# Attention of an encoder block with the keys instead of the queries on the partitions

## The chip, the cores and the metric

The kernel runs on one NeuronCore of a Trainium2 chip. Five engines work side by side and meet through semaphores: TensorE (PE in the rows; its weight loads are PEld), VectorE (DVE), ScalarE (ACT), GpSimd (POOL) and SyncE (SP), which only issues DMAs. The metric is the device time of one execution in microseconds, the median of several.

## What is computed

One layer over two independent sequences, a sample of 2048 tokens and a prompt of 256, all in float32, with 1024 columns. Cut to what matters:

```python
hdn = rmsnorm(x, norm_pre)
u, b_gate, c_gate, z_conv, q_lat, kv_lat, k_pe, z_attn = split(hdn @ w_in)
conv_out = b_gate * short_conv(c_gate * u) * silu(z_conv)            # 512 columns
q = rmsnorm(q_lat) @ w_uq        # 8 heads of 64 + 32 columns, the 32 rotated
k, v = rmsnorm(kv_lat) @ w_ukv   # 8 heads of 64 + 64; the 32 rotated key columns are shared
sc = q @ k.T / sqrt(96)          # per head and sequence
o = softmax(sc) @ v * silu(z_attn)
y = x + rmsnorm(concat(conv_out, o) @ w_out, norm_post)
```

## The kernel before

It works in four parts.

**Phase 1** (`phase1`) makes the latents, the convolution branch and the attention's gate. Its products are float32r, in three passes: each operand is cut into a rounded part and a rest, and `mm3` (L87 to 93) adds hi*hi, lo*hi and hi*lo.

**Phase 2** (`Phase2.run`, L531) goes through nine chunks of 256 tokens, the prompt first. Each chunk makes keys, values and queries from the latents with float16 parts, in PSUM groups of 256 columns (keys 4, queries 6) or 512 (values 2), cuts each result into two float16 parts (`split`: ScalarE L71, then VectorE L72) and stores both to DRAM scratch with DMAs on SP: keys (L567, and L594 for the rotated rows, copied to all heads), values (L597), queries (L567). `Heads.load` (L634 on) reads a head's operands back.

**Attention** (`attention`, L655 on) takes 130 units one after the other: two for the prompt, then, head by head, 128 queries of the sample against all 2048 keys. `step(n)` (L847 on) writes the order out by hand (`manual_schedule`): scores of unit n, parts of units n-1 and n-2, value products of the pair of units six steps back (`LAG`). In a unit:

- `scores`: 12 float16 products of 512 columns with the queries on the partitions, into one PSUM tile of 1024 columns and two of 512; VectorE takes the maxima (L695) and forms their negative in one column (L700, L701);
- `exponents`: ScalarE's exponentials with that column as bias, and the row sums (L717), into float32 tiles `p`;
- `upper`, `lower`: `p` is cut into two float16 parts `fp`, by POOL (L756, L759), ScalarE (L758) and VectorE (L765);
- L771: a DMA turns both parts round, into `tt` with the keys on the partitions;
- `values`: 2 float16 products (L775, L776) of 256 columns for each 128 keys and pair of units. The weights are the value's two parts side by side, 128 columns; the stream is the exponentials' first, then second part. `finish` adds the two halves (L833, L839) and stores.

One over the sums goes to DRAM as rows (`spread`, L742 to 747).

**Phase 4** (`Phase4`) is the output projection, for 18 tiles of 128 tokens in two halves of 512 columns, 24 float32r products each (L955, L957). Before that the attention's rows are scaled with the gate and the sums (L935, L937) and cut (L939, L941). Its first halves run between the last steps of the attention.

The exponentials come out with the queries on the partitions, and everything from `upper` to L771 is there to turn them for the value products:

```python
nc.scalar.activation(p, s, AF.Exp, bias=sm[:, 0:1], scale=g.exps[:, 0:1], accum_out=sums[h][:, i, u : u + 1])
```

Of the kernel before, what the change touches and what calls it, by code (L numbers as in the profile page):

```python
# [10 lines left out]
F32 = mybir.dt.float32  # L11
# [28 lines left out]
BIG = 2.0**15  # L40
# [3 lines left out]
LN_BIG = float(np.log(BIG))  # L44
# [3 lines left out]
GROUP, LAST = 4, 2  # L48
LAG = 6
CUT = 384  # L50
# at which step of a head what of the next one is loaded
LOADS = {3: ("k", 0, 1024), 5: ("k", 1024, TS), 7: ("q", 0, 1024), 9: ("q", 1024, TS), 11: ("v", 0, 1024), 13: ("v", 1024, TS)}
# [11 lines left out]
def split(nc, hi, lo, src, scale=None):  # L64
    """hi is src rounded to the products' type, lo what is left; scale goes on both."""
# [21 lines left out]
def mm3(nc, out, terms, first=True, last=True):  # L87
    """float32 products from parts: hi*hi + hi*lo + lo*hi."""
# [7 lines left out]
def rstd(g, r, ssq, n):  # L96
    """r = (ssq / n + eps) ** -0.5 on a column."""
# [5 lines left out]
def phase1(g, x, x_t, w_e, w_lat, npre, convw, open_phase2):  # L103
    """Norm, latents, the conv branch and the attention's gate."""
    nc, tc = g.nc, g.tc
    with ExitStack() as ctx:
# [15 lines left out]
        # The products take x times the norm's weights; a token's scale goes on what comes out of them.  # L122
# [43 lines left out]
        def spread(hf):  # L166
            """The scales of a half's tokens along the free axis, on every partition."""
# [8 lines left out]
        def latents(tiles, between=lambda k: None):  # L176
            """Products of some tokens' tiles, normalised."""
# [64 lines left out]
        def etile(n):  # L242
# [3 lines left out]
            for ci in range(3):  # L246
# [13 lines left out]
                # columns of cu: the sample's end and the prompt's start lie a zero apart  # L260
# [34 lines left out]
        def conv(hf, j, ci):  # L295
            # output tokens of this step: those whose right neighbour is there
# [7 lines left out]
            for a, b in spans:  # L304
                # column of token a in cu
# [79 lines left out]
class Phase2:  # L385
    """Queries, keys and values from the latents, 256 tokens at a time, the prompt first.

    They are stored as two float16 parts each, after powers of two that bring them within the type's range:
    one over what goes on a query's row goes on the key's, but for a factor that is the same for all rows.
    """  # L390

    N = 256

    def __init__(self, g, table):
# [3 lines left out]
        self.turn = 3  # L398
# [255 lines left out]
def attention(g, hd, ps1):  # L654
# [106 lines left out]
    def lower(n, b):  # L761
# [4 lines left out]
        if b == 0:  # L766
            return
# [385 lines left out]
```

## Time and profile before

| | us |
|---|---|
| median of 3 runs | 1746.72 (1746.57 to 1747.05) |
| the profiled execution, its span | 1753.0 |
| PE busy, weight loads busy | 1577.4, 1254.1 |
| DVE, ACT, POOL busy | 1085.1, 821.2, 787.3 |
| phase 1 | 0 to 644.4 |
| phase 2, until its last product | 644.4 to 761.5 |
| attention, until its last scores | 761.5 to 1523.0 |
| overlap of its end with phase 4 | 1523.0 to 1559.3 |
| phase 4 alone | 1559.3 to 1753.0 |

The profile holds one execution. Its only time of its own is the span from the first to the last instruction, 6.3 us above the median of the timed runs. Busy shares of the whole span mix stages with different limits, so they are read stage by stage. A matmul's busy time is longer than the distance to the next one, since matmuls are pipelined: what a product costs in a row of products is the distance between two starts.

### The profile page before, as it was taken

The numbers are of one execution on the slowest core, as the hardware profiler recorded it, in microseconds if no ns is written. First come the engines' busy times: TensorE is split into PE (matmuls) and PEld (weight loads), VectorE is DVE, ScalarE is ACT, GpSimd is POOL, SyncE is SP. The second block draws the span as 40 slices with busy tenths as digits, with TensorE's granted clock in tenths as the row PEclk, the third lists the DMA queues.
The fourth block names the chain that finished last, engine by engine and source line by source line (L and its number), as shares of the span: only waits on it lengthen the run. The fifth ranks groups of instructions, "written<-read, shape, count | busy, mean of one in ns | idle before, by whom it ended". The sixth has DMA issues, their size and how long they took to land.

```text
span 1753.0 us, 24925 instructions
## 1 busy us (share of the span) xinstructions
PE 1577.4 (90%) x9168; PEld 1254.1 (72%) x9168; DVE 1085.1 (62%) x1679; ACT 821.2 (47%) x1596; POOL 787.3 (45%) x785
## 2 busy tenths in 40 slices
PE   8999999999999999978788788888887887889998
PEld 8999999999999997644444444445454444567886
DVE  4333332322444435588799999899999999823333
ACT  7521112452112223367676777677766767612221
POOL 3221121131322113346667676677767677722232
PEclk9999999999999999999899999999999999989999
DMA  9921112543212239999999999999999999994663
GB/s 285 287 78 42 58 50 89 159 108 125 82 60 86 83 114 243 268 197 215 200 209 218 212 221 196 224 205 229 206 224 190 222 206 214 203 226 154 191 192 109
DMA packets 695503, 301.45 MB, mean 172 GB/s; under 512 B 570322, under 2 KB 665428, under 8 KB 695380
## 3 DMA queue, kind: packets, MB, share of 16 engines
q1 hardware_dynamic: 676164, 271.53, 69.4%
q10 hardware_dynamic: 19216, 28.32, 6.4%
q8 instruction: 72, 1.18, 0.3%
q14 instruction: 51, 0.42, 0.1%
HBM read 108.84 MB, written 48.74 MB: 90 GB/s over the span
## 4 chain that ended last, share of the span: by engine, by line
PE 55%; DVE 30%; DMA 7%; ACT 3%; POOL 2%; issue 2%; ACTq 0%; SPq 0%; DVEq 0%; POOLq 0%
DVE mx L695 12%; PE o L91 10%; PE o L93 9%; PE o L92 9%; DVE fp L765 9%; PE out L955 7%; DVE sm L700 7%; DMA tt<-fp 5%; PE out L957 3%; PE pq L91 1%; PE pq L92 1%; PE pq L93 1%; ACT p L717 1%; PE o L775 1%; DMA k_s<-krp 1%
## 5 line engine op out<-in xcount | busy, mean ns | idle before, releaser
L717 ACT ACTIVATE p<-s,sm,exps 128x512 f32<-128x512 f32 (+1 forms) x384 | 348.6, 914 | 184.6 <-DVE sm L701 167.9
L759 POOL TENSOR_TENSOR fp<-p,fp 128x640 f16<-128x640 f32 x260 | 377.4, 1471 | 11.9 <-ACT fp L758 1.1
L775 PE MATMUL o<-tt,v 128*128 128x256 f16 x1024 | 253.8, 285 | 115.5 <-DVE res L839 113.1
L695 DVE TENSOR_REDUCE mx<-s 128x1 f32<-128x512 f32 (+1 forms) x384 | 320.4, 856 | 17.3 <-PE s L93 16.4
L91 PE MATMUL o<-hdn_hi,whi 128*128 128x384 f32 x960 | 323.7, 337 | 0.0
L92 PE MATMUL o<-hdn_lo,whi 128*128 128x384 f32 x960 | 322.7, 336 | 0.0
L93 PE MATMUL o<-hdn_hi,wlo 128*128 128x384 f32 x960 | 322.6, 336 | 0.0
L776 PE MATMUL o<-tt,v 128*128 128x256 f16 x1024 | 252.6, 284 | 0.0
L765 DVE TENSOR_TENSOR fp<-p,fp 128x384 f16<-128x384 f32 x260 | 236.3, 909 | 12.8 <-POOL fp L756 12.6
L756 POOL TENSOR_SCALAR fp<-p 128x1024 f16<-128x1024 f32 x130 | 143.6, 1105 | 219.5 <-ACT p L717 143.1
L91 PE MATMUL s<-k,q 96*128 96x512 f16 (+1 forms) x528 | 210.9, 399 | 28.2 <-ACT p L717 25.1
L776 PEld LDWEIGHTS <-v 128*128 128x128 f16 x1024 | 104.5, 102 | 168.5 <-issue 136.9
L93 PE MATMUL s<-k,q 96*128 96x512 f16 (+1 forms) x528 | 211.0, 400 | 0.0
L92 PE MATMUL s<-k,q 96*128 96x512 f16 (+1 forms) x528 | 209.9, 398 | 0.0
L91 PEld LDWEIGHTS o<-hdn_hi,whi 128*128 128x128 f32 x960 | 180.5, 188 | 0.5
L92 PEld LDWEIGHTS o<-hdn_lo,whi 128*128 128x128 f32 x960 | 180.5, 188 | 0.0
L93 PEld LDWEIGHTS o<-hdn_hi,wlo 128*128 128x128 f32 x960 | 180.5, 188 | 0.0
L758 ACT ACTIVATE fp<-p 128x1024 f16<-128x1024 f32 x130 | 137.4, 1057 | 29.7 <-DMA tt<-fp 26.2
L955 PE MATMUL out<-wo,o_cut 128*128 128x512 f32 x576 | 144.0, 403 | 7.9 <-ACT o_cut L939 7.5
L775 PEld LDWEIGHTS <-v 128*128 128x128 f16 x1024 | 104.0, 102 | 49.4 <-issue 10.7
L700 DVE SCALAR_TENSOR_TENSOR sm<-mx 128x1 f32<-128x1 f32 x128 | 132.4, 1034 | 4.5
L955 PEld LDWEIGHTS out<-wo,o_cut 128*128 128x128 f32 x576 | 109.2, 191 | 34.5 <-ACT o_cut L939 8.2
(222 smaller groups left out, 2227.9 us busy)
## 6 DMA issues: line engine op xcount, KB each, us to landing
w<-in_w_e_dram SPq DMA_DIRECT2D x40, 512.0 KB
x<-in_x_dram SPq DMA_DIRECT2D x18, 512.0 KB
out_dram<-yt SPq DMA_DIRECT2D x36, 256.0 KB
xt<-in_x_t_dram SPq DMA_DIRECT2D x5, 1536.0 KB
o_raw<-mix_s SPq DMA_DIRECT2D x15, 512.0 KB
o_raw<-in_x_dram SPq DMA_DIRECT2D x15, 512.0 KB
lat_s<-lt SPq DMA_DIRECT2D x6, 960.0 KB
lt<-lat_s SPq DMA_DIRECT2D x9, 640.0 KB
```

Source lines behind the costliest of these rows:

```text
L91: nc.tensor.matmul(out, sh, mh, start=first and i == 0, stop=False)
L92: nc.tensor.matmul(out, sh, ml, start=False, stop=False)
L93: nc.tensor.matmul(out, sl, mh, start=False, stop=last and i == n - 1)
L695: nc.vector.reduce_max(mx[:, at : at + 1], s, axis=AX.X)
L700: nc.vector.scalar_tensor_tensor(sm[:, 8:9], mx[:, 0:1], mx[:, 2:3], mx[:, 3:4], op0=ALU.max, op1=ALU.max)
L717: nc.scalar.activation(p, s, AF.Exp, bias=sm[:, 0:1], scale=g.exps[:, 0:1], accum_out=sums[h][:, i, u : u + 1])
L756: nc.gpsimd.tensor_scalar(hi, p, 1.0, 1.0, op0=ALU.mult, op1=ALU.mult)
L759: nc.gpsimd.tensor_tensor(lo[:, CUT:], p[:, CUT:], hi[:, CUT:], op=ALU.subtract)
L765: nc.vector.tensor_tensor(lo[:, :CUT], p[:, :CUT], hi[:, :CUT], op=ALU.subtract)
L775: nc.tensor.matmul(o, v, moving[0], start=first, stop=False)
L776: nc.tensor.matmul(o, v, moving[1], start=False, stop=last)
L955: nc.tensor.matmul(o, mh[:, k, :], wk[k // 2][:, k % 2, w], start=k == 0 and wk is hi, stop=False)
```

## The change

The attention is written anew, and the stages around it follow.

- **Phase 2** makes the keys of all chunks first (after the prompt's keys and queries), then two chunks of queries, then all values, then the other queries. Values stay in SBUF as float32 (`g.v`), with no parts and no way through DRAM. The prompt's attention, and the maxima of the first group, run between the groups of the values and the later queries.
- **Attention**: a group is 512 queries of two heads (16 groups), a step is 128 keys of them (256 steps). `scores` forms the products with the keys on the partitions: 6 float16 products of 512 columns, 3 for each head, into a 1024-column tile. The softmax's maximum is a 97th row of the queries (its partner in the keys is a row of 2^14), so the exponential needs no bias and comes out ready for the value products.
- **Maxima** of group n+1 are taken during group n, from the products of the operands' first parts alone: 32 more products of 512 columns for a group, 2 or 3 in a step, each into one of two PSUM banks (`m`) and reduced by VectorE. `max_rows` turns them into rows with 8 products of 128 columns, which ScalarE copies into the queries.
- **Value products** are float32, one for each head and 128 keys, 64 weight columns and 512 columns of stream, one head's result on partitions 0 to 63, the other's on 64 to 127. They are issued for four steps together.
- **Sums**: POOL adds up the exponentials over the steps (`total`); two float32 products with ones bring the sums onto the partitions of the result, VectorE inverts them, and gate and sums are applied in the attention (`finish`), not in phase 4.
- **Phase 4** starts when the attention ends, takes whole tiles of 1024 columns, and loads and cuts only.

```diff
 class Attention:
+    def max_chunks(self, n):
...
+        for u in range(8):
+            i, b = divmod(u, 4)
+            for c in range(4):
+                m = g.narrow(f"m{n}_{u}_{c}", "m")
+                nc.tensor.matmul(m, q[:DQK, i, 0, b * P : (b + 1) * P], k[:DQK, i, 0, c * 512 : (c + 1) * 512], start=True, stop=True)
+                nc.vector.reduce_max(mx[:, u, c : c + 1], m, axis=AX.X)
+                yield
+    def max_rows(self, n):
...
+            for b in range(4):
+                nc.tensor.matmul(m[:KR, b * P : (b + 1) * P], mst[:, (4 * i + b) % 8, :KR], self.ident, start=True, stop=True)
...
+            nc.scalar.activation(dst, src.rearrange("p (h t) -> p h t", t=TP) if n == "p" else src, AF.Copy)
+    def scores(self, s, k, q, pieces):
+        o = g.wide(f"s{s}")
+        for cols, ki, qi, ks in pieces:
+            nc.tensor.matmul(o[:, cols], k[:KR, ki, 0, ks], q[:KR, qi, 0, :], start=True, stop=False)
+            nc.tensor.matmul(o[:, cols], k[:DQK, ki, 0, ks], q[:DQK, qi, 1, :], start=False, stop=False)
+            nc.tensor.matmul(o[:, cols], k[:DQK, ki, 1, ks], q[:DQK, qi, 0, :], start=False, stop=True)
+    def exponents(self, s, o):
+        p = self.p[s] = self.ps.tile([P, 1024], F32, tag="p", bufs=6, name=f"p{s}")
+        nc.scalar.activation(p, o, AF.Exp, scale=g.exps[:, 0:1])
+    def total(self, key, first, second=None):
...
+            nc.gpsimd.tensor_tensor(self.acc[key], self.acc[key], first, op=ALU.add)
+    def finish(self, key, j, cols):
...
+            nc.tensor.matmul(r[i * DV : (i + 1) * DV, :w], self.ones, acc[:, i * w : (i + 1) * w], start=True, stop=True)
+        nc.scalar.activation(rs, r[:, :w], AF.Copy)
+        yield
+        for i in range(0, w, P):
+            nc.vector.reciprocal(rs[:, i : i + P], rs[:, i : i + P])
...
+        nc.vector.tensor_tensor(res, o[:, :w], gate, op=ALU.mult)
+        nc.sync.dma_start(g.mix[CW + j * P : CW + (j + 1) * P, cols], res)
+    def step(self, s):
...
+        o = self.scores(s, self.k[j], self.q[n], pieces)
+        for _ in range(3 if kt % 4 == 0 else 2):
+            next(self.ahead, None)
+        if n < last:
+            if kt == KT - 3:
+                next(self.ahead, None)
+                self.max_columns(n + 1)
+            if kt == KT - 2:
+                self.max_rows(n + 1)
+        if s % BATCH == 1:
+            self.values(range(max(s - BATCH, 0), s))
...
+        self.exponents(s, o)
+        if kt == 1:
+            self.total(n, self.p[s - 1], self.p[s])
+        elif kt:
+            self.total(n, self.p[s])
+        self.settle()
+    def values(self, steps):
...
+                nc.tensor.matmul(self.o[n][i * DV : (i + 1) * DV], g.v[:, kt, h * DV : (h + 1) * DV], p[:, i * 512 : (i + 1) * 512], start=kt == 0, stop=kt == KT - 1)
...
-            nc.gpsimd.tensor_tensor(lo[:, CUT:], p[:, CUT:], hi[:, CUT:], op=ALU.subtract)
-        nc.vector.tensor_tensor(lo[:, :CUT], p[:, :CUT], hi[:, :CUT], op=ALU.subtract)
-        nc.sync.dma_start_transpose(dst, parts.pop(n).rearrange("p w k -> p (w k)"))
-        nc.tensor.matmul(o, v, moving[0], start=first, stop=False)
-        nc.tensor.matmul(o, v, moving[1], start=False, stop=last)
```

In the middle of the attention, PE's row before (`s65` are scores of unit 65, `o58` the outputs of the pair 58 and 59):

```order
L93 MATMUL s65_0_10739<-k_3_9094,q_3_9093 128x512
L775 LDWEIGHTS v_3_9095
L775 MATMUL o58_10702<-tt58_10476,v_3_9095 128x256
L776 LDWEIGHTS v_3_9095
L776 MATMUL o58_10702<-tt58_10476,v_3_9095 128x256
L775 LDWEIGHTS v_3_9095
L775 MATMUL o58_10702<-tt58_10476,v_3_9095 128x256
L776 LDWEIGHTS v_3_9095
L776 MATMUL o58_10702<-tt58_10476,v_3_9095 128x256
```

and PE's row after, at step 5 (`s5`, `s6` are scores of steps, `m1` products for the next group's maxima, `p1` to `p4` exponentials of steps 1 to 4):

```order
L778 LDWEIGHTS k_0_6296
L778 MATMUL s5_7596<-q_0_6482,k_0_6296 128x512
L741 LDWEIGHTS q_1_7485
L741 MATMUL m1_3_0_7603<-k_0_6296,q_1_7485 128x512
L741 LDWEIGHTS q_1_7485
L741 MATMUL m1_3_1_7606<-k_0_6296,q_1_7485 128x512
L885 MATMUL o0_7538<-p1_7541,v_5674 64x512 x2
L885 MATMUL o0_7538<-p2_7558,v_5674 64x512 x2
L885 MATMUL o0_7538<-p3_7574,v_5674 64x512 x2
L885 MATMUL o0_7538<-p4_7593,v_5674 64x512 x2
L776 LDWEIGHTS k_0_6296
L776 MATMUL s6_7620<-q_0_6482,k_0_6296 128x512
```

Value products no longer stand in eights between a unit's scores: eight float32 ones follow every fourth step's scores and maxima, and carry their weight loads in themselves.

VectorE's row before, one unit (`mx` maxima, `sm` their column, `fp` the float16 parts):

```order
L765 TENSOR_TENSOR fp53_10144<-p53_0_10129,fp53_10144 128x384
L695 TENSOR_REDUCE mx55_10187<-s55_0_10189 128x1
L765 TENSOR_TENSOR fp53_10144<-p53_1_10130,fp53_10144 128x384
L695 TENSOR_REDUCE mx55_10187<-s55_1_10213 128x1
L695 TENSOR_REDUCE mx55_10187<-s55_2_10214 128x1
L700 SCALAR_TENSOR_TENSOR sm55_10188<-mx55_10187 128x1
L701 TENSOR_SCALAR sm55_10188<-sm55_10188,exps_75 128x1
L839 TENSOR_TENSOR res46_2_10096<-o48_10152,top48_3_10233 64x256
```

and after, in the second group's steps 7 to 10 (`m2` products for the third group's maxima, `rsum0` the first group's sums):

```order
L742 TENSOR_REDUCE mx2_7826<-m2_3_3_7956 128x1
L808 RECIPROCAL rsum0_7944<-rsum0_7944 128x128
L742 TENSOR_REDUCE mx2_7826<-m2_4_0_7970 128x1
L742 TENSOR_REDUCE mx2_7826<-m2_4_1_7973 128x1
L808 RECIPROCAL rsum0_7944<-rsum0_7944 128x128
L742 TENSOR_REDUCE mx2_7826<-m2_4_2_7987 128x1
L742 TENSOR_REDUCE mx2_7826<-m2_4_3_7990 128x1
L742 TENSOR_REDUCE mx2_7826<-m2_5_0_7993 128x1
```

The parts, the columns for the bias and the sum of halves have left VectorE; reductions and inversions stay.

SP's row before, one chunk of phase 2 (`sk`, `krp`, `sv`, `sqp`, `sq` are its keys, rotated keys, values, rotated queries, queries):

```order
L567 DMA k_s_67<-sk4_6366 64x8x256 x2
L594 DMA k_s_67<-krp4_6417 32x8x256 x2
L597 DMA v_s_68<-sv4_6407 128x8x256
L567 DMA q_s_66<-sqp4_6368 32x4x256 x4
L567 DMA q_s_66<-sq4_6432 64x8x256 x2
```

and after, in the stretch of the keys (chunks 3 to 5; the rows have no queries between them):

```order
L568 DMA tb5_32_6085<-in_table_dram 32x2x256
L586 DMA kp5_6087<-kpe_s_61 32x256
L601 DMA k_s_66<-krp3_6008 32x8x256 x2
L576 DMA k_s_66<-sk3_5990 64x8x256 x2
L601 DMA k_s_66<-krp4_6061 32x8x256 x2
L576 DMA k_s_66<-sk4_6043 64x8x256 x2
L601 DMA k_s_66<-krp5_6114 32x8x256 x2
L576 DMA k_s_66<-sk5_6095 64x8x256 x2
```

The stores of all keys now follow one another, the stores of the values are gone.

## Rows read from the trace of the kernel before

**Rows 1.** Busy us by engine, granted clock and DMA share, in five stretches.
```profile
core 0: us, PE busy (x) PEld busy (x) DVE busy (x) ACT busy (x) POOL busy (x), PEclk, DMA share, GB/s
0.00:644.40 644.40, 638.18 (x3804) 635.96 (x3804) 228.42 (x379) 188.52 (x371) 140.73 (x251) 1.00 0.35 111
644.40:761.50 117.10, 105.93 (x836) 82.41 (x835) 69.08 (x193) 48.91 (x123) 37.73 (x51) 0.99 0.96 253
761.50:1523.00 761.50, 617.27 (x3572) 363.86 (x3570) 705.38 (x986) 534.62 (x1002) 542.40 (x406) 0.93 1.12 211
1523.00:1559.30 36.30, 28.76 (x129) 22.31 (x129) 15.01 (x22) 9.23 (x18) 12.64 (x11) 0.86 1.22 215
1559.30:1753.00 193.70, 187.26 (x832) 149.57 (x832) 67.18 (x100) 39.93 (x86) 53.75 (x67) 0.99 0.53 167
```
**Rows 2.** Groups by line and shape, VectorE, 800 to 1500: busy us, mean ns.
```profile
L765 DVE TENSOR_TENSOR fp<-p,fp 128x384 f16<-128x384 f32 x236 | 212.8, 902 | 5.9 <-POOL fp L756 5.9
L695 DVE TENSOR_REDUCE mx<-s 128x1 f32<-128x512 f32 x236 | 152.5, 679 | 15.2 <-PE s L93 14.6
L695 DVE TENSOR_REDUCE mx<-s 128x1 f32<-128x1024 f32 x118 | 142.9, 1211 | 0.9 <-PE s L93 0.7
L700 DVE SCALAR_TENSOR_TENSOR sm<-mx 128x1 f32<-128x1 f32 x118 | 124.7, 1057 | 4.2
```
**Rows 3.** Waits, 800 to 1500: us in total, times, longest.
```profile
ACT p L717 <- DVE sm L701: 161.8, 97, 3.0
PE o L775 <- DVE res L839: 113.1, 58, 5.4
```
**Rows 4.** Chain that ended last, phase 4: start, us, sixteen products of one half.
```profile
1735.38 3.74 PE out L955 x16
```
**Rows 5.** Timeline of PE in a unit's scores: start, us, instruction.
```profile
1100.37 0.38 PE L91 MATMUL s<-k,q 96*128 96x512 f16 x1
1100.59 0.38 PE L92 MATMUL s<-k,q 96*128 96x512 f16 x1
```
**Rows 6.** Timeline of PE around the prompt's value products, 64 weight columns.
```profile
779.17 0.38 PE L93 MATMUL s<-k,q 96*128 96x512 f16 x1
779.48 0.30 PE L91 MATMUL o<-tt,v 128*64 128x256 f16 x1
...
780.70 0.27 PE L93 MATMUL o<-tt,v 128*64 128x256 f16 x1
780.90 0.39 PE L91 MATMUL s<-k,q 96*128 96x512 f16 x1
```
**Rows 7.** Groups by shape, ScalarE's exponentials of 1024 columns, 800 to 1500.
```profile
L717 ACT ACTIVATE p<-s,sm,exps 128x1024 f32<-128x1024 f32 x119 | 142.1, 1194 | 0.0
```
**Rows 8.** Groups by shape, VectorE's inversions, 800 to 1753.
```profile
L731 DVE RECIPROCAL rs<-rs 128x16 f32<-128x16 f32 x7 | 1.8, 253 | 0.2
L731 DVE RECIPROCAL rs<-rs 128x4 f32<-128x4 f32 x1 | 0.2, 178 | 0.0
```
**Rows 9.** Groups by shape, POOL's two-operand passes over float32, whole span.
```profile
L941 POOL TENSOR_TENSOR o_cut<-o_raw,o_cut 128x1024 fp32r<-128x1024 f32 x18 | 43.5, 2416 | 140.7 <-ACT o_cut L939 140.7
L1053 POOL TENSOR_TENSOR wo<-stw,wo 128x512 fp32r<-128x512 f32 x16 | 22.4, 1400 | 0.0
```
**Rows 10.** Groups by shape, PE in phase 2: a third of the queries', of the keys'.
```profile
L91 PE MATMUL q<-lt,uq_hi 128*128 128x256 f16 x162 | 44.9, 277 | 7.9 <-DVE sv L72 5.8 <-DVE sqr L543 1.9
L91 PE MATMUL k<-lt,uk_hi 128*128 128x256 f16 x72 | 19.6, 273 | 3.3 <-DVE sq L72 3.3
```
**Rows 11.** Timeline of SP in phase 2: start, us to issue, which DMA.
```profile
706.25 0.59 SPq L529 DMA_DIRECT2D kp<-kpe_s  x1
706.93 1.25 SPq L567 DMA_DIRECT2D k_s<-sk  x2
708.28 2.06 SPq L594 DMA_DIRECT2D k_s<-krp  x2
```
**Rows 12.** Chain that ended last: a load of phase 4, until its data are there.
```profile
1550.10 5.36 DMA o_raw<-mix_s
```

More of the change, by code (lines that the diff above doesn't have):

```diff
@@ new lines, in queries @@
+                    yield "q", ci, m
+            last = len(self.chunks)
+            self.load(1, pb, "q")
+            yield from keys(0)
+            yield from queries(0)
+            self.load(2, pb, "q")
+            for ci in range(1, last):
+                yield from keys(ci)
+            for ci in (1, 2):
+                yield from queries(ci)
+                self.load(ci + 2, pb, "q")
+            for ci in range(last):
+                yield from values(ci)
+            for ci in range(3, last):
+                yield from queries(ci)
+                if ci + 2 < last:
+                    self.load(ci + 2, pb, "q")
@@ L905, in __init__, with load @@
         self.ready = {}
[L906 to L911 removed]
+    def load(self, i):
+        nc = self.g.nc
         sl = slice(i * P, (i + 1) * P)
[L913 to L926 removed]
@@ L1032, in tile_encoder, with beside @@
-    hd.load(0, "v", 1536, TS)
-    hd.load(0, "q", 1536, TS)
-    g.pb = pool("p3b", bufs=2)
+    side = []
+    def beside():
+        yield from at.max_chunks("p")
+        at.max_columns("p")
+        yield
+        at.max_rows("p")
+        yield
+        first = at.max_chunks(0)
+        rest = [at.prompt(j) for j in range(H // 2)]
+        live = [rest.pop(0)]
+        for i, _ in enumerate(first):
+            yield
+            if i % 2 == 0 and live:
+                if next(live[0], at) is at:
+                    live.pop(0)
+                    live += rest[:1]
+                    del rest[:1]
+        at.max_columns(0)
+        yield
+        at.max_rows(0)
+        yield
+        for w in live + rest:
+            for _ in w:
+                yield
@@ L1035, in tile_encoder @@
+    for _ in between:
+        pass
     pwo = pool("p4w", bufs=1, side="right")
@@ L1101, in tile_encoder @@
-    for n in range(NU, NU + LAG + 1):
-        step(n, more=more)
-    while halves:
-        more()
+    p4 = Phase4(g, at, x, (wo[:4], wo[4:]), y)
+    steps = 2 * H * KT
+    for s in range(steps):
+        at.step(s)
+        k, i = divmod(s - 8, 28)
+        if 0 <= k < 8:
+            spare(k, i)
+        if s == steps - 12:
+            g.post = at.ps.tile([P, D], F32, tag="st", bufs=1, name="g_post")
+            nc.sync.dma_start(g.post, npost)
+    tiles = [16, 17, *range(16)]
+    p4.load(tiles[0])
@@ L1107, in _layout, with ahead @@
+    p4.load(tiles[1])
+    p4.split(tiles[0])
+    at.end(steps)
+    for n, i in enumerate(tiles):
+        def ahead():
+            if n + 1 < len(tiles):
+                p4.split(tiles[n + 1])
+            if n + 2 < len(tiles):
+                p4.load(tiles[n + 2])
+        p4.run(i, ahead)
 def _layout(i):
```

735 lines of the change are left out of this document (302 added, 433 removed).

## The prediction

> **What bounds the kernel now.** First the busy times by stretch [rows 1]. Phase 1, to 644.4, is full of products (PE 638.2 of 644.4) and is not touched. Phase 2 takes 117.1 with PE at 105.9 and the DMA engines at 0.96: both are near their limit. In the attention VectorE is busy for 705.4 of 761.5, PE for 617.3 at a mean granted clock of 0.93, ScalarE and POOL for some 540. Phase 4 alone is PE again, 187.3 of 193.7. So the attention waits for VectorE, and the groups show with what [rows 2]: of 700 us, 212.8 go to the second float16 parts, 295.4 to the maxima, 124.7 to one-column instructions that take a microsecond each. The waits agree [rows 3]: the exponentials wait 161.8 for the column of maxima, the value products 113.1 for VectorE's sum. PE, which has the most to do elsewhere, stands idle here by turns.
>
> The prices on PE are distances between starts. In phase 4 sixteen products of 512 columns take 3.74, 0.234 each [rows 4]; a half is 24 of them, 5.62, and all 36 halves 202.3. After 1559.3 there is room for 187.3 / 5.62 = 33.3 halves until PE's end, so 2.7 halves (15 us) lie in the 797.8 from 761.5 to 1559.3. The attention itself is then 783 for 130 units, 6.0 each.
>
> **The change part by part.** VectorE's parts, its one-column work and its sums of halves go; so do POOL's and ScalarE's parts and the turning DMAs. What is late next is PE, whose work grows. I price one group (16 steps, as much as 8 old units, 48 us before).
>
> Scores: 96 float16 products of 512 columns, as before. Maxima: 32 more. Each is 0.216 [rows 5], so 128 are 27.6. They take their stationary operand with a separate load as before; those loads lie under the streams.
>
> Value products: 32 float32 ones, 16 pairs. No row shows such a product. From below, phase 4's products read four-byte operands in one stream: 0.234 [rows 4]. From above: the kernel before reaches float32 from float16 parts with all four part products, two in 128 weight columns, two streams; in 64 weight columns that is four streams of 512, 4 x 0.216 = 0.864 [rows 5]. And a pair may run at once, in two halves of the array, or one after the other. So a pair is worth 0.234 to 1.73. I take 0.864, the price of the kernel before for the same accuracy: a group then streams 16 x 4 x 512 columns, as many as eight units' value products did (8 x 16 x 2 x 128). That is 13.8 a group; the row-sum product with ones is one more pair, 0.9.
>
> [...]
>
> Switching to 64 weight columns and back is in the prompt's products: from 779.17 to 779.48 is 0.31 where 0.216 would do, from 780.70 to 780.90 0.20 where the 256-column rows stand 0.108 apart [rows 6]. So 0.09 each way; five batches a group, 0.9. Eight products of 128 columns for the rows of maxima: 0.4, at a quarter of 0.216 each.
>
> Waits that the change adds. The maxima have two banks, and VectorE's reduction of one takes 0.679 [rows 2]. Every fourth step has three: the first product is complete 0.38 after its start [rows 5], its reduction ends at 1.06, and PE wanted the bank at 0.43. That is 0.63 with all scores and value products queued behind it on PE, four times a group, 2.5; the row-sum product takes one of the two banks too, and holds it until ScalarE's copy behind an exponential of 1.19 [rows 7], another 1.2. At the end of a group two copies of rows go ahead of an exponential on ScalarE; the next group's first scores need that exponential's PSUM tile: two copies of half its length, 1.2, and 1.19 of its own against 1.3 of PE's work, 1.1. Together 4.8.
>
> A group is 27.6 + 13.8 + 0.9 + 0.9 + 0.4 + 4.8 = 48.4, no less than before. Fifteen of these and a last one without maxima, 37: 763. I take 770, for the hand-overs between engines.
>
> The others stay below that. VectorE has 32 x 0.679 + 4 inversions of 128 columns, each 178 + 124 x (253 - 178) / 12 = 950 ns [rows 8], and little else: 27. ScalarE has 16 x 1.19 and three copies: 22. POOL has 15 additions of 1024 columns at 2.42 when alone or 2 x 1.40 beside VectorE [rows 9], with gate and weights 39 to 45. Nearest is POOL; it decides from (48.4 - 3) / 15 = 3.0 an addition.
>
> Phase 2. PE's products there are 162 x 3 and 72 x 3 of 256 columns [rows 10] and 108 of 512: 99 us, unchanged. The prompt comes to it with 11: 48 score products at 0.108 are 5.2, the rest value products, maxima and sums. What moves is SP's work. A chunk's keys are 2.6 on PE, but 1.25 + 2.06 for the stores and twice 0.59 for small loads on SP [rows 11]: 4.5. Before, queries and values of the same chunk covered that; now eight chunks of keys follow one another, 36 instead of 21, and the loads of keys behind them wait on SP for the stores to land. The first group's maxima are 32 x 0.679 = 21.7 on VectorE beside the later queries, of which some 8 is not covered. Against it the values' parts on VectorE, their store and their reload go. 117 + 15 + 8 + 11 less about 11 for the values: 140, with 117 and 165 as ends.
>
> Phase 4: 202.3 of products as before, none of them overlapped now. A tile's load is issued when the tile two before has left VectorE, some 4 after its products; 5.4 for the data [rows 12] and 1.1 for the cut make 10.5 of the 11.2 that the tile between takes, so I give 3 for refills (15 at most). Last tile and beginning: 10.
>
> Sum: 644.4 + 140 + 770 + 202.3 + 3 + 10 = 1770 against the profiled 1753.0, 1.0% more. The profile stands 6.3 above the median of the runs, so 1764 against 1746.7.
>
> **The rivals.** *A, the forecast:* four streams, a pair at once, 1764. Its own range is 1714 to 1825: below, half of the bank waits (35) and phase 2 at 117; above, phase 2 at 165, refills at 15, and a clock that stays at 0.93 for part of the attention. [...]
>
> *B, the pair runs one after the other.* The change then does not do what its two tiles are for. A group gains 13.8 + 0.9, sixteen of them 235: 1999. For it: no row shows two tiles at work, and each float32 product may hold the whole array for its streams. Against it: the two write different partitions and read different columns, and nothing in the order keeps them apart.
>
> *C, the float32 product needs fewer streams: faster than before.* With two streams, 17 pairs a group save 0.432 each, 117 in all: 1647. With one, as in phase 4 [rows 4], POOL's 39 takes over, and it ends near 1626. C decides from 17 us over 272 pairs on, that is from 0.80 a pair; above that the kernel is not faster. For it: phase 4's products read four-byte operands in one stream. Against it: those are float32r, and phase 1 and 4 add up three of them for the precision that this one product is to have.
>
> [...]
>
> *D, POOL.* At 3.3 an addition a group is 15 x 0.3 longer, 72 in all. It is near A's upper end and has its chance there; for it speaks only that POOL is slower beside VectorE [rows 9], against it that VectorE now reads PSUM and writes one column.
>
> **How the numbers follow.** A has 0.60, B 0.25, C 0.15. Within A, 17 us above the median before with a spread of some 28, I put 0.14 on faster, 0.05 on the same, 0.41 on slower. With C faster is 0.29, with B slower 0.66; the bound is 0.2%, 3.5 us, about what a measurement of this kernel can tell from no change. The range goes from 1700, which leaves out most of C, to 2020, which takes in most of B; some 0.2 is left out. The predicted time is A's, 1764.
>
> **What the profile after would show.** Two value products (L885) that start nearly together, and pairs 0.86 apart: A; 1.73 apart: B; 0.43 or less: C. PE waits for VectorE's reductions (L742) of some 60 in all and for exponentials of some 18 at the groups' ends; if these are absent, the waits were wrong. VectorE busy for about 0.55 of the attention instead of 0.93. First sample scores near 785, attention 770 long, then phase 4 in tiles of 11.2 without gaps. What would make it wrong: value products at another price than 0.864 a pair, a keys' stretch without SP in the way (117 for phase 2), or a clock that falls in the value products.

## The result and the profile after

| | before | after | forecast |
|---|---|---|---|
| median, us | 1746.88 (1746.57 to 1749.65) | 1884.15 (1882.64 to 1886.22) | 1764 |
| ratio to before, 95% interval | | 1.078 (1.0765 to 1.0795) | 1.010 |
| phase 2, until the first sample scores (before: until its last product) | 117.1 | 261.9 | 140 |
| attention, from there to the first output product | 797.8, with 15 of phase 4 | 765.1 | 770 |
| phase 4 from there on | 193.7 | 209.7 | 215 |

The change makes the kernel 7.8% slower. The forecast had the sign, but the 120 us between 1764 and 1884 lie in one stage: phase 2 takes 122 us more than forecast, the other stages 10 less, and the rest is the forecast's allowance of 6 us between profile and median, which here goes 3 the other way. That allowance was no property of the kernel: in the runs of this document the span lies some 2 us under the time of the same execution (1881.1 and 1882.9 here), so the profiled execution of the kernel before was by an estimate one of some 1755 us, slower than its median. In the kernel after, phase 2 also holds the prompt's attention and the first group's maxima.

The busy times by stretch of the kernel after, cut where the cells of [rows 1] were cut (phase 2, attention up to the last scores, hand-over, phase 4):

```profile
core 0: us, PE busy (x) PEld busy (x) DVE busy (x) ACT busy (x) POOL busy (x), PEclk, DMA share, GB/s
644.40:906.30 261.90, 148.45 (x980) 101.44 (x980) 93.33 (x228) 56.85 (x124) 47.74 (x62) 0.80 0.42 112
906.30:1661.70 755.40, 703.41 (x3209) 268.72 (x3207) 376.04 (x587) 315.38 (x317) 597.91 (x272) 1.00 0.10 31
1661.70:1671.40 9.70, 5.04 (x18) 1.07 (x16) 0.00 (x0) 2.39 (x3) 9.47 (x5) 0.88 0.33 108
1671.40:1881.10 209.70, 202.39 (x866) 162.65 (x864) 49.25 (x41) 38.57 (x54) 55.55 (x55) 0.99 0.38 127
```

In the attention PE has become the bound, as forecast: busy for 703 of 755 at a granted clock of 1.00. VectorE fell from 0.93 of the stretch to 0.50. Phase 2 is the odd row: PE is busy for 148 of 262, the DMA engines are at 0.42 where [rows 1] has 0.96, the granted clock is at 0.80. Nothing there is full; everybody waits.

PE in the attention, from the timeline (start, us, instruction), around one batch of value products:

```profile
1205.50 0.38 PE L741 MATMUL m<-k,q 96*128 96x512 f16 x1 [0.57 <-DVE mx L742]
...
1207.02 0.59 PE L741 MATMUL m<-k,q 96*128 96x512 f16 x2
1207.54 3.65 PE L885 MATMUL o<-p,v 128*64 128x512 f32 x16
1211.03 1.03 PE L803 MATMUL r<-acc,ones_f 128*64 128x512 f32 x4
```

Four pairs take 3.49 from start to start, 0.87 a pair. The trace records each float32 product as two MATMULs, so a batch of eight is x16. The groups of the attention, by shape (busy us, mean ns, then idle time before them and its releaser):

```profile
L885 PE MATMUL o<-p,v 128*64 128x512 f32 x1024 | 234.1, 599 | 0.0
L776 PE MATMUL s<-q,k 97*128 97x512 f16 x512 | 195.0, 381 | 11.5 <-ACT p L784 11.5
L741 PE MATMUL m<-k,q 96*128 96x512 f16 x480 | 148.0, 378 | 40.4 <-DVE mx L742 40.4
```

And the chain of waits through phase 2, at its longest hole:

```profile
748.89 14.97 SPq L699
763.90 16.88 DMA tb<-in_table_dram
780.88 0.44 DVE sqr L561
781.36 0.37 PE q L91
```

SP stood 15 us in the issue of one load of head pair 0's keys (L699), and the table behind it, which the rotation of the second sample chunk's queries needs, took 17 us to land. In the run with the rows apart (below) tables of this size, 256 KB, land in 4.4 (median of nine). PE stood idle for 25.83, and its products behind the hole are slow at first (granted clock 0.50 from 781.4 to 785.1, then 1.00):

```profile
781.36 0.37 PE L91 MATMUL q<-lt_q,uq_hi 128*128 128x256 f16 x1 [25.83 <-DVE sqr L561]
781.52 0.42 PE L92 MATMUL q<-lt_q,uq_hi 128*128 128x256 f16 x1
781.74 0.42 PE L93 MATMUL q<-lt_q,uq_lo 128*128 128x256 f16 x1
...
785.12 0.27 PE L91 MATMUL q<-lt_q,uq_hi 128*128 128x256 f16 x1
785.23 0.27 PE L92 MATMUL q<-lt_q,uq_hi 128*128 128x256 f16 x1
```

### The profile page after: what moved, and what is told of

Read it like the earlier page. It is cut to its first block, busy times and chain, and to the rows that moved or that the text cites. A ratio compares the mean times of both kernels' runs of the same rounds, so it can differ in the third digit from the quotient of the medians.

```text
span 1881.1 us, 22488 instructions
## 1 busy us (share of the span) xinstructions
PE 1697.6 (90%) x8870; PEld 1170.3 (62%) x8870; DVE 747.1 (40%) x1234; ACT 601.7 (32%) x868; POOL 852.9 (45%) x647
## 4 chain that ended last, share of the span: by engine, by line
PE 80%; DVE 7%; DMA 3%; ACT 3%; SPq 2%; issue 2%; POOL 2%; DVEq 0%; POOLq 0%; ACTq 0%
PE o L885 12%; PE o L91 9%; PE o L92 9%; PE o L93 9%; PE out L929 7%; PE s L776 5%; PE m L741 5%; PE s L777 5%; PE s L778 5%; DVE mx L742 4%; PE out L931 3%; PE pq L91 1%; PE pq L92 1%; PE pq L93 1%; DVE rsum L808 1%
## 5 line engine op out<-in xcount | busy, mean ns | idle before, releaser
L794 POOL TENSOR_TENSOR acc<-acc,p 128x1024 f32<-128x1024 f32 x224 | 526.4, 2350 | 147.3 <-ACT p L784 135.4
L742 DVE TENSOR_REDUCE mx<-m 128x1 f32<-128x512 f32 x512 | 325.7, 681 | 354.4 <-PE m L741 354.4
L784 ACT ACTIVATE p<-s,exps 128x1024 f32<-128x1024 f32 x256 | 283.6, 1113 | 317.7 <-PE s L778 296.8
L91 PE MATMUL o<-hdn_hi,whi 128*128 128x384 f32 x960 | 323.6, 337 | 0.0
L885 PE MATMUL o<-p,v 128*64 128x512 f32 x1024 | 234.1, 599 | 0.0
L776 PE MATMUL s<-q,k 97*128 97x512 f16 x512 | 195.0, 381 | 11.5 <-ACT p L784 11.5
L741 PE MATMUL m<-k,q 96*128 96x512 f16 x512 | 159.7, 378 | 45.1 <-DVE mx L742 44.9
L777 PE MATMUL s<-q,k 96*128 96x512 f16 x512 | 194.3, 379 | 0.0
L778 PE MATMUL s<-q,k 96*128 96x512 f16 x512 | 193.1, 377 | 0.0
L91 PEld LDWEIGHTS o<-hdn_hi,whi 128*128 128x128 f32 x960 | 180.5, 188 | 0.5
L885 PEld LDWEIGHTS o<-p,v 128*64 128x64 f32 x1024 | 67.7, 136 | 136.6 <-issue 136.3
L776 PEld LDWEIGHTS <-k 97*128 97x128 f16 x512 | 49.1, 96 | 153.9 <-issue 109.2
L777 PEld LDWEIGHTS <-k 96*128 96x128 f16 x512 | 50.2, 98 | 65.8 <-issue 16.5
```

Of the source, the lines that this page charges most:

```text
L91: nc.tensor.matmul(out, sh, mh, start=first and i == 0, stop=False)
L741: nc.tensor.matmul(m, q[:DQK, i, 0, b * P : (b + 1) * P], k[:DQK, i, 0, c * 512 : (c + 1) * 512], start=True, stop=True)
L742: nc.vector.reduce_max(mx[:, u, c : c + 1], m, axis=AX.X)
L776: nc.tensor.matmul(o[:, cols], k[:KR, ki, 0, ks], q[:KR, qi, 0, :], start=True, stop=False)
L777: nc.tensor.matmul(o[:, cols], k[:DQK, ki, 0, ks], q[:DQK, qi, 1, :], start=False, stop=False)
L778: nc.tensor.matmul(o[:, cols], k[:DQK, ki, 1, ks], q[:DQK, qi, 0, :], start=False, stop=True)
```

## The experiments

The theory that these rows suggest, W: the loads of the keys have become 97 rows high, for the row of 2^14, and such a load runs on one of the 16 DMA engines; SP and the transfers behind it stand still. The rival, O: the order in blocks (all keys, then values, then queries) is what costs, whatever the loads. The kernel before was run beside each; its median lay between 1746.9 and 1752.8 from chip to chip, so runs on different chips are compared by their ratio to it.

| run | median | ratio to before | first sample scores at |
|---|---|---|---|
| the change | 1884.15 | 1.078 (1.0765 to 1.0795) | 906.3 |
| rows apart | 1834.47 | 1.049 (1.0459 to 1.0521) | 855.1 |
| rows apart, banks | 1813.92 | 1.036 (1.0335 to 1.0386) | 837.1 |
| rows apart, chunk by chunk | 1799.24 | 1.027 (1.0238 to 1.0302) | 817.3 |
| rows apart, chunk by chunk, banks | 1774.85 | 1.0143 (1.0115 to 1.017) | 792.4 |
| all edits | 1735.52 | 0.9916 (0.9898 to 0.9935) | 792.3 |

### The height of the key loads

**Rows apart** (`e1_rows_apart`):

```diff
-            for w, n in ((0, KR), (1, DQK)):
-                nc.sync.dma_start(t[:n, i, w], g.k[w, h, :n, cols])
+            for w in range(2):
+                nc.sync.dma_start(t[:DQK, i, w], g.k[w, h, :DQK, cols])
+            nc.sync.dma_start(t[DQK:KR, i, 0], g.k[0, h, DQK:, cols])
```

> The keys' 97th row (of 2**14) is loaded by a DMA of its own, the other 96 rows by one as before. Theory W (width): a load of 97 rows is carried by one of the 16 DMA engines (20 to 31 GB/s where the 97-row loads ran alone, at 754 to 764 us of the changed kernel's trace), and what SP issues behind it waits; k_p's load costs 15 us of phase 2, k_0's two some 33, k_1's two 20 to 28: the time falls by 50 to 75 us, to 1810 to 1835, and the loads land in under 4 us. Theory O (order): phase 2 is long because the keys, values and queries are made in blocks and SP's queue stands in another order; the width is nothing, and the time stays within 1875 to 1890.

1834.47, so 50 us less, at the upper edge of W's range. One part of W's expectation was missed: the loads of 96 rows land after 6.7 (median of sixteen), not in under 4. SP's timeline around head pair 0's keys, in the change

```profile
742.97 20.89 SPq L699 DMA_DIRECT2D k<-k_s  x4
763.90 4.97 SPq L568 DMA_DIRECT2D tb<-in_table_dram  x2
```

and with the rows apart

```profile
728.18 1.76 SPq L700 DMA_DIRECT2D k<-k_s  x4
729.98 6.15 SPq L568 DMA_DIRECT2D tb<-in_table_dram  x2
```

The four loads of the rows are issued in 1.76 instead of 20.89. What the DMA engines did meanwhile in the change, 748 to 764 in 40 slices (share in tenths, then GB/s), and the row of its middle by engines:

```profile
DMA  7789200000000000000000000000000000000000
GB/s 154 195 317 318 62 10 31 20 31 20 31 20 31 31 20 31 20 31 20 31 20 31 31 20 31 20 31 20 31 31 20 31 20 31 20 31 20 31 31 20
752.00:763.00 11.00, 3.11 (x27) 2.63 (x27) 2.35 (x6) 1.20 (x3) 0.00 (x0) 0.76 0.06 26
```

The last two numbers are the mean share of the 16 DMA engines and the GB/s. A share of 0.06 is one engine's worth of sixteen, and in the trace's transfers of this stretch nearly always only one is under way at a time (for 0.98 of 752 to 763).

**97 rows in the kernel before** (`e2_before_97`) puts the height, and nothing else, into the other kernel:

```diff
+            n = DQK + (kind == "k" and h == 0)
-            self.queue.dma_start(dst[:DQK, :, cols], src[:, h * DQK : (h + 1) * DQK, cols]...)
+            self.queue.dma_start(dst[:n, :, cols], src[:, h * DQK : h * DQK + n, cols]...)
```

> The kernel before with its three sample loads of head 0's keys in phase 2 made 97 rows high (the extra row is the next head's first, and is not used); SP's order is the same. Theory W: 388 KB for each 1024 columns on one engine at 25 GB/s, some 31 us of one-engine transfer in all, of which at least the last load (194 KB, 7.8 us, just ahead of the first sample scores) is on the path: 1755 to 1780, and a stretch with a DMA share under 0.1 in phase 2 where there was none. Theory O: 1745 to 1750.

1776.25 against 1750.02, ratio 1.016 (1.0126 to 1.0193). The extra row is 1% of the data and costs 26 us. **98 rows** (`e8_before_98`) is the same line with `2 *` ahead of the bracket:

> The kernel before with its three loads of head 0's keys in phase 2 98 rows high instead of 96 (and instead of the 97 of the earlier run). [...] Theory H (any height that isn't 96, or no multiple of 16 or 32, goes to one engine): as with 97, 1770 to 1781.

1749.9 against 1747.3, ratio 0.9998 (0.997 to 1.0026): nothing, where theory H has 1770 to 1781. The first of these loads, 715 to 735 in 40 slices, and the row of 719 to 726, with 97 rows

```profile
DMA  6399998000000000000000009589899799972000
GB/s 131 71 176 170 168 269 199 8 12 25 29 16 25 29 25 25 25 29 25 25 25 29 25 25 147 127 322 410 334 348 307 180 315 239 255 207 66 25 25 29
719.00:726.00 7.00, 5.90 (x44) 3.99 (x42) 3.35 (x10) 2.30 (x7) 1.53 (x2) 1.00 0.06 24
```

and with 98:

```profile
DMA  8864999998989997799999999999999999999966
GB/s 214 185 128 82 176 165 174 269 222 97 227 332 318 334 274 229 277 320 357 268 228 225 315 344 346 343 345 349 330 376 367 316 268 211 174 214 316 217 129 188
719.00:726.00 7.00, 6.32 (x47) 4.36 (x46) 3.35 (x10) 2.38 (x7) 2.29 (x4) 1.00 1.00 265
```

With 97 rows the share is one engine's worth of sixteen (0.06), with 98 it is full (1.00, other transfers included). So not every height but 96 is slow, nor every one that is no multiple of 16 or 32: theory H fails. No other height of these loads was run, and why 97 rows are slow where 96 and 98 are not, no run shows.

### The value products

**One tile** (`e3_one_tile`): both heads' products go to the same 64 weight columns, so the heads are summed together, and what the attention needs, one result for each head, is left out. Behind the products both halves of the result are read from these 64 rows (not shown). It is a single execution.

```diff
-nc.tensor.matmul(self.o[n][i * DV : (i + 1) * DV], ..., start=kt == 0, stop=kt == KT - 1)
+nc.tensor.matmul(self.o[n][:DV], ..., start=kt == 0 and i == 0, stop=kt == KT - 1 and i == 1)
```

> The changed kernel with both heads' value products in columns 0 to 63, into the same 64 rows (so the heads are summed together; the output differs). Theory A (two column tiles run side by side, a pair 0.87 us): the products follow one another, a pair takes 1.7 to 1.75 us, 256 of them 0.86 more each: 1884 + 220, 2080 to 2115. Theory C (a float32 product costs 0.43 us by itself, the tiles do nothing): 1875 to 1890.

2100.71, 217 more, 0.85 for each of 256 pairs, as theory A has it. Four pairs by PE's timeline:

```profile
1308.80 7.08 PE L889 MATMUL o<-p,v 128*64 128x512 f32 x16
1315.81 0.39 PE L776 MATMUL s<-q,k 97*128 97x512 f16 x1
```

1.75 a pair, against 0.87 in two tiles: one float32 product of 512 columns takes 0.87, four times a float16 one's 0.216 [rows 5], and the two tiles of the change do run at once.

### The waits for the maxima

**Between** (`e4_between`): one maximum's product goes between a step's score halves.

```diff
-        for cols, ki, qi, ks in pieces:
+        for at, (cols, ki, qi, ks) in enumerate(pieces):
+            if at:
+                next(between, None)
```

> The changed kernel with one maximum's product between a step's two halves of scores and the rest behind the second half, where two or three stood behind it in a row. If PE's 44.9 us of waits for the maxima are a matter of spacing (a bank comes free 0.68 us after its product ended, and the next but one product comes sooner): the waits fall under 15 us and the time to 1845 to 1860. Rival: the exponentials take the time back, since the scores end later by one product each (0.22 us a step, the exponents' own waits 11.5 us grow by as much): 1875 to 1890.

1852.21, 31.9 less; the attention until its last scores fell from 755 to 723. The group of these products, whose waits were 44.9 over the whole span:

```profile
L741 PE MATMUL m<-k,q 96*128 96x512 f16 x512 | 189.0, 377 | 16.4 <-DVE mx L742 16.1
L778 PE MATMUL s<-q,k 97*128 97x512 f16 x512 | 195.1, 381 | 11.6 <-ACT p L786 11.6
```

28.8 of the 31.9 are these waits (44.9 to 16.1), and the scores' wait for the exponentials is what it was (11.5 in the change). So most of the waits were a matter of spacing; 16.1 stay, where the expectation had under 15.

### The order in phase 2

With the rows apart phase 2 is still 210.7. Three patches of the blocks followed. **Late loads** (`e5_late_loads`) takes most of the 16 latent loads off SP's queue ahead of the first chunk's table, **values beside** (`e6_values_beside`) mixes the value products into the next chunk's keys, **all three** (`e7_all`) adds the maxima between the halves:

```diff
-            for ci in range(1, len(self.chunks)):
-                self.load(ci, pb, "kv")
...
+                if ci + 3 < last:
+                    self.load(ci + 3, pb, "kv")
+                v = values(ci - 1)
+                for i, what in enumerate(keys(ci)):
+                    yield what
+                    if i % 2:
+                        yield next(v)
```

> The rows apart, as in the run before, and of the 16 loads of the keys' and values' latents that stood first in phase 2 (8.4 us of SP's issue at 646 to 654.5 us) all but two chunks' issued later, behind the first chunk's table and rotated keys. Theory Q (SP's queue sets the opening: PE sat idle 14.5 us at 648.9 to 663.3 until the rotated keys came): 8 to 14 us less than the run with the rows apart, 1820 to 1827. Rival: the same loads then stand between the key chunks' stores and take the gain back there: 1831 to 1837.

> As the run with the late loads, and each chunk's value products between the products of the next chunk's keys, as the kernel before has them side by side, where they stood in one block of 28 us in which the DMA share was 0.00; the prompt and the first maxima go with queries 1 to 8. Theory B (blocks: keys alone wait for stores and tables, values alone leave the DMA engines empty): 25 to 40 us less than with the late loads, 1783 to 1802; PE's busy share from 690 us on over 0.85. Rival: keys are paced by their stores at 5.2 us a chunk whatever PE does beside them, and the queries with all the maxima get longer by as much: 1815 to 1830.

> As the run with the values beside the keys, and one maximum's product between a step's score halves. If the gains are of separate stages they add: 31.9 us less, by what this edit brought alone (1884.2 - 1852.2); with theory B 1751 to 1771. Rival: with phase 2 shorter another wait in the attention's first groups takes part of it: over 1771.

1839.16, 1824.94 and 1790.24. The late loads gained nothing. PE's hole of 14 us at 649 to 663 was down to 3.9, but PE's timeline has one of the old size behind it, where the next table now stands behind the prompt's loads (only the products that end a wait):

```profile
660.13 0.27 PE L91 MATMUL q<-lt_q,uq_hi 128*128 128x256 f16 x1 [0.93 <-DVE sq L72]
664.17 0.27 PE L91 MATMUL q<-lt_kv,uk_hi 128*128 128x256 f16 x1 [0.93 <-DVE sq L72]
683.06 0.37 PE L91 MATMUL k<-lt_kv,uk_hi 128*128 128x256 f16 x1 [16.77 <-DVE sk L72]
```

The values beside the keys brought 14 (the expectation had 25 to 40; the time is in its rival's range), the maxima 35 on top, about as much as alone; all three stay above the 1751 to 1771 of theory B. **Prompt later** (`e9_prompt_later`) moved those loads behind the fourth chunk's keys, **more buffers** (`e10_more`) added a third buffer in four places (and gave the latents of keys and values four in turn) and put the first output tile ahead of the last row sums:

```diff
-        if (kind, ci, m) == ("q", 0, 3):
+        if (kind, ci, m) == ("k", 4, 3):
             at.load_q("p")
```

> As the run with all three edits, and the prompt's queries and keys (1.5 MB) are loaded behind the fourth chunk's keys instead of right behind the first queries. In the runs with the late loads PE sat idle 16 us (665 to 681 us) because chunk 1's table and rotated keys were issued behind these loads. Theory Q (that issue order is what took the late loads' gain back): 12 to 18 us less than the run with all three edits (1790), 1770 to 1780. Rival (the DMA engines are full there and somebody waits in any order; the hole moves to 720 to 740 us): 1786 to 1792.

> As the run with the prompt later, with a third buffer for tables, rotated keys, their parts and the keys' and queries' stores (the latents of keys and values rotate through four in exchange), and with the first output tile's products ahead of the last row sums' (PE idled 4.7 us there). Theory: 4 to 5 us at the end, 4 to 10 in phase 2: 8 to 15 under the run with the prompt later, 1756 to 1772. Rival (phase 2 is by now PE's own work of some 145 to 150 us at the granted clock): 3 to 5 less only.

1793.96 and 1795.53. By its ratio, 1.0236 against 1.0238 with all three, the first gained nothing, as its rival has it. The second gained nothing either, less than the 3 to 5 of its own rival. PE's busy time in the old hole rose, and fell at the new place of the prompt's loads. By stretches, all three and then prompt later with more buffers (prompt later alone has PE at 7.30 and 5.32):

```profile
665.00:681.00 16.00, 2.26 (x15) 1.30 (x14) 1.40 (x5) 0.77 (x2) 1.20 (x2) 0.64 0.95 214
702.00:715.00 13.00, 8.50 (x43) 4.76 (x41) 3.38 (x11) 3.11 (x7) 3.06 (x4) 0.74 0.52 124
665.00:681.00 16.00, 7.11 (x39) 4.21 (x37) 3.80 (x12) 3.27 (x9) 3.06 (x4) 0.79 0.56 140
702.00:715.00 13.00, 0.93 (x5) 0.43 (x4) 1.87 (x6) 0.98 (x2) 1.53 (x2) 0.73 0.65 152
```

So the hole went where the large loads went. **Chunk by chunk** (`e11_chunkwise`) gives the blocks up: keys, values and queries of a chunk in turn, inputs two chunks ahead with one table for a chunk instead of two, a third buffer for the stores, the operands of the attention in pieces between, the prompt and the maxima beside the later chunks; `e12_chunkwise_all` adds the maxima between the halves and the first output tile ahead of the last sums.

```diff
+            for ci in range(last):
+                for i in (1, 2) if ci == 0 else (ci + 2,):
+                    for what in ("kv", "q", "tb") if i < last else ():
+                        self.load(i, pb, what, 3)
+                yield from keys(ci)
+                yield from values(ci)
+                yield from queries(ci)
```

> The rows apart (1834.5), and phase 2 in the kernel before's order: each chunk's keys, values and queries in turn, its latents, one table and rotated keys loaded two chunks ahead (three buffers), the prompt's operands and head pair 0's keys loaded in pieces between; the prompt's attention goes beside chunks 4 to 6 and the first group's maxima beside chunks 7 and 8, a quarter of them behind the last chunk. Theory B (the blocks of keys, values and queries make the loads and stores come in bursts, and PE idles in each: 60 of some 205 us in the patched versions): phase 2 falls from 211 us to the kernel before's 117 plus 20 to 35 for the prompt and the maxima, 1765 to 1785. Rival (the prompt's and the maxima's hand-overs between engines are what costs, in any order): 1815 to 1840.

> As the run chunk by chunk, with one maximum between a step's score halves (31.9 us by itself) and the first output tile's products ahead of the last row sums' (4.7 us of PE's idle time in the versions without). Theory B: 1728 to 1750, so level with the kernel before (1747) or a little under it. Rival: 1778 to 1805.

1799.24 and 1764.76, each between the two ranges that were expected. Phase 2 fell from 210.7 to 172.9, so the order costs, but the expectation of 137 to 152 was not reached. Whether the early loads did it, **one ahead** (`e16_one_ahead`) tells; it has the banks of the next section and is to be read against 1774.85:

```diff
-                for i in (1, 2) if ci == 0 else (ci + 2,):
+                for i in (ci + 1,):
...
-                        self.load(i, pb, what, 3)
+                        self.load(i, pb, what, 2)
```

> As the run chunk by chunk with the banks changed (1774.9), but with two buffers and the loads of the next chunk asked for at the start of the present one; on SP's queue they then stand behind the present chunk's stores. Theory E (early loads are what the order chunk by chunk lives on): PE waits 3 to 6 us for its operands at each of eight chunks, 25 to 50 us more, 1800 to 1825. Theory M (the mixture of keys, values and queries is): under 10 us more, 1774 to 1785.

1775.98, ratio 1.0142 against 1.0143, and the first sample scores stand 2 later (794.4): theory M, the early loads are worth next to nothing. That leaves the mixture of keys, values and queries, with what came with it in one edit: half as many tables, the pieces of the attention's operands, the new places of the prompt and the maxima. These were not taken apart. Third buffers and a later prompt had gained nothing on the blocks.

### Two groups in one PSUM tile

PE's timeline of the run chunk by chunk shows what was left (only the products that end a wait):

```profile
658.96 0.27 PE L91 MATMUL q<-lt_q,uq_hi 128*128 128x256 f16 x1 [0.93 <-DVE sq L72]
663.01 0.27 PE L91 MATMUL k<-lt_kv,uk_hi 128*128 128x256 f16 x1 [1.27 <-DVE sk L72]
666.07 0.38 PE L91 MATMUL k<-uv_hi,lt_kv 128*128 128x512 f16 x1 [0.93 <-DVE sk L72]
670.65 0.27 PE L91 MATMUL q<-lt_q,uq_hi 128*128 128x256 f16 x1 [0.85 <-DVE sqr L561]
```

About every third group waits a whole eviction (the time that ScalarE and VectorE take to read a group's results out of PSUM). It is the group in the second half of the two-bank tile (`bank`): its first product waits until the first half has been read. In the kernel before each group has a tile of its own. **Banks** (`e14_chunkwise_banks`; `e15_banks` on the blocks; `e13_banks_all` with all edits):

```diff
-                if self.turn % 3 == 0:
-                    return g.narrow(name, "o")
-                if self.turn % 3 == 1:
-                    self.pair = g.wide(name)
-                half = self.turn % 3 - 1
-                return self.pair[:, half * 512 : (half + 1) * 512]
+                return g.wide(name)[:, :512] if self.turn % 2 else g.narrow(name, "o")
```

> The run chunk by chunk (1799), with phase 2's products of one group each in a tile of their own: the two-bank tile is used by its first half alone, in turn with the one-bank tiles, so four groups in flight where there were six. Theory T (the changed kernel puts two groups into one two-bank tile, and the second half's first product waits until the first half has been read, 0.85 to 1.27 us at each of 36 pairs): 25 to 35 us less, 1764 to 1776, and PE's waits for L72 and L561 in phase 2 fall from 34 us to under 8. Rival (the evictions on ACT and DVE are the pace, and with fewer banks in flight PE waits as long at the next bank): 1795 to 1805.

> The same edit of the banks on the kernel with the rows apart and the blocks kept (1834.5). Theory T with SP's stores pacing the key block: only the queries and values gain, 8 to 18 us, 1816 to 1827. If the tile halves were behind the key block's pace too, 25 to 35 us, 1800 to 1810. Rival: 1830 to 1840.

> The run chunk by chunk with all edits (1764.8), with the banks as in this call's first run, the second part of the first output tile cut by DVE instead of POOL (PE waited 3.1 us for it), and two maxima a beat beside the last queries. Theory T: 28 to 40 us less, 1725 to 1737, under the kernel before (1747 to 1752). Rival: 1755 to 1768.

1774.85, 1813.92, 1735.52: theory T each time, on the blocks 2 under its range. The third run has two small edits more than the banks (its expectation names them), so its 29 are not the banks' alone. PE's waits in phase 2 (total, times, longest), chunk by chunk:

```profile
PE k L91 <- DVE sk L72: 20.5, 18, 2.3
PE q L91 <- DVE sq L72: 7.5, 8, 1.2
PE q L91 <- DVE sqr L561: 5.8, 9, 0.8
```

and with the banks:

```profile
PE m_p L736 <- DMA k_p<-k_s: 9.6, 1, 9.6
PE m L723 <- DVE mx L724: 5.4, 10, 1.1
PE k L91 <- DVE sk L72: 0.6, 2, 0.3
```

33.8 us of waits became 0.6, with four groups in flight instead of six. Phase 2 is 25 shorter, less than that: PE now reaches the prompt's maxima 9.6 before the prompt's keys are there, and the wait for the maxima's banks went from 1.9 to 5.4.

**All edits** is 0.84% faster than the kernel before (ratio 0.9916, 0.9898 to 0.9935). By stretches (phase 2 but for its last half microsecond, attention until the last score product has started, the rest):

```profile
644.40:791.70 147.30, 128.21 (x981) 92.69 (x980) 91.21 (x229) 55.46 (x124) 48.08 (x62) 0.97 0.71 190
791.70:1518.30 726.60, 702.53 (x3210) 269.21 (x3208) 396.65 (x585) 315.95 (x318) 597.57 (x272) 1.00 0.11 33
1518.30:1733.20 214.90, 206.47 (x884) 163.27 (x882) 50.51 (x42) 41.30 (x57) 64.05 (x58) 0.99 0.38 129
```

PE is busy for 0.87, 0.97 and 0.96 of them: 19 us of its idle time are left in phase 2, 24 in the attention, 8 in the rest.

## Why the prediction was wrong

**What bounds the attention**, and what becomes its bound: right. VectorE was the limit, and PE is it now.

**Value products, 0.864 a pair:** right, 0.87 measured. Rival B (one after the other) did not happen; the run with one tile shows its price, 1.75. Rival C did not happen: a float32 product of 512 columns takes 0.87, four times a float16 one's 0.216, also in one tile, where a pair takes 1.75. That a pair runs at once was an assumption of the sum, which no row of the kernel before shows; 0.87 against 1.75 shows it.

**Waits in the attention, 4.8 a group:** right in kind, a little too large. The maxima cost 40.4 in the attention where some 60 were forecast, the exponentials 11.5 where 18 were. The three maxima in a row were the main cause, as spacing them showed. That the attention comes out at 765 against 770 is in part luck: without its waits the sum has some 691, and PE's own work took 703, which made up for half of what the waits fell short.

**POOL** (rival D): 2.35 an addition, under the 3.0 from which it would decide.

**Phase 4:** right. In PE's timeline a half's sixteen and eight products take 3.74 and 1.86 and follow one another without a gap, so the 3 for refills was not needed.

**Phase 2, 140:** this step failed, by 122. It named the right place, SP in the stretch of the keys, and priced it from what SP takes to issue the same DMAs in the kernel before [rows 11]. Three things were not in the sum.

- The loads of 97 rows. The step counts SP's stores and small loads at their old price and has the key loads only wait for the stores, with no price of their own; but the change had altered their height, and the DMAs of [rows 11] and [rows 12] are 32, 64 and 128 rows high. Undone, it gives back 51 of phase 2 (906.3 to 855.1) and 50 of the time.
- The order in blocks. I had it as 15 us of SP's issue. By the run chunk by chunk, with all that its edit holds, it costs 38 (855.1 to 817.3) on the way taken here, 45 with the banks changed first (837.1 to 792.4): the key block waits for its tables and stores while PE idles, the value block has PE at work and the DMA engines at a share of 0.00 (760 to 788 in the run with the rows apart). Moving single loads only moved the holes.
- The tile halves. The step took the products of phase 2 as "unchanged" at 99 us. They are; but `bank` now puts two groups into one tile, and the second waits for the first's eviction. That is 25 chunk by chunk, 18 in the blocks. The waits of 0.9 to 1.3 at L91 stand in the change's own timeline too, and the new `bank` is in the kernel after, though not in the part of the diff shown ahead of the prediction.

With these three undone phase 2 is 148.0. Without its 15 for SP the step would have said 125, so its other terms (maxima, prompt, values) are 23 short together. Of these 9.6 are one wait for the prompt's keys. PE is busy there for 128.5, 22.6 more than in [rows 1], where the step adds 19 for the prompt and the maxima; whether the 11 that it takes off for the values came is not measured. The upper end that I gave phase 2, 165, was drawn from the same issue times, so the range held the time by luck: it reached up for rival B, which had nothing to do with it. (A's own lower end, 1714, is also 8 above its terms: 1764 less 35 less 23 is 1706.)

## What to carry to other kernels

A change of a tile's height is a change of the DMA that fills it: before a load keeps its old price, compare its partition count with that of the loads the price was read from. In the kernel before 97 rows cost 26 us and 98 cost nothing; in the change, splitting off the odd row gave back 50. Phase 2 was near two limits at once, and mixing its kinds of work did more for it than moving single loads; a reordering into blocks has to be priced by who idles in each block, not by the issue times alone. Two groups of products in the two halves of one PSUM tile waited here for each other's eviction (33.8 us in phase 2, chunk by chunk), and with a tile each they did not (0.6), so give each group its own.

## What the runs showed of the hardware

- A load of 97 rows keeps one engine's worth of the 16 DMA engines busy (share 0.06, 24 GB/s at 719 to 726); with 98 rows the share is 1.00 in the same stretch, at 265 GB/s, other transfers included. SP's issue stops meanwhile: four loads take 20.89, two of them 97 rows high, instead of 1.76. One row more costs the kernel before 26 us, and a second one takes that back.
- A float32 product of 512 columns with 64 weight columns takes 0.87, is recorded as two MATMULs, and two of them in two tiles of 64 columns take 0.87 together; in one tile they take 1.75.
- The granted clock of phase 2 was 0.80 in the change and 0.98 chunk by chunk. Behind the hole of 25.83 the products of 256 columns stand 0.21 apart until 785, at a granted clock of 0.50, and 0.11 apart from there on, at 1.00. For the same products PE is busy for 148 in the change and 133 chunk by chunk, so by an estimate from these two the low clock lengthens the stage by up to 15.
